# Sixteen start places for the hi and lo halves of the weights, one for each group of products

## The chip, the cores and the metric

The kernel runs on one core of one Trainium2 chip. The metric is the device time of one execution in microseconds (us); lower is better. Two executions of the kernel before took 2779.8 and 2778.5 us, median 2779.15 us. A further execution was recorded by the hardware profiler.

## What is computed

Two transformer blocks of width 2048 over 256 tokens, one after the other, each followed by its own feed-forward part. Cut to what matters here, everything is a chain of dense products with some work between them:

```python
# block 1 (x: [1, 256, 2048], all float32)
mod = silu(c) @ ada_w + ada_b                         # six vectors of 2048: shifts, scales, gates
h = rms_norm(x, g) * (1 + sc1) + sh1
u, lru_gate, q, k, v, mix_gates = split(h @ w_in + b_in)
y_lru  = rg_lru(conv(u)) * gelu(lru_gate)             # scan over the tokens
y_attn = sliding_window_attention(q, k, v, sinks)     # window 128, 16 heads, 4 kv heads
merged = sig(m0) * (y_lru @ w_lru_out) + sig(m1) * (y_attn @ w_attn_out)
x = x + g1 * (merged @ w_o)
h2 = rms_norm(x, g) * (1 + sc2) + sh2
x = x + g2 * ((silu(gate) * up) @ w_ffn_out)          # gate, up = h2 @ w_ffn_in
x = rms_norm(x, final_g)
# block 2
x = x + gla_mixer(rms_norm(x), gla_w_in, ..., gla_w_out)
x = x + swiglu(rms_norm(x), ffn_w_gu, ffn_w_down)
```

## The kernel before

**Products.** All weights are float32 in HBM, packed in chunks of 512 x 512 (1 MB, a tile `raw` of 128 partitions x 4 x 512). The large products do not run as full float32 matmuls: each operand is split into a rounded half `hi` (type float32r) and the rest `lo = raw - hi`, and three float32r matmuls, hi·hi, hi·lo and lo·hi, are added up in PSUM. `split` (L157) does this for the weights of one chunk: one DMA on the SyncE queue (SP), then for each half of the chunk one ScalarE copy to `hi` (L165) and one VectorE subtraction to `lo` (L167), 128 x 1024 elements each. `hi`, `lo` and `raw` rotate through three buffers each. The activations are held already split, as pairs of tiles (class `Pair`); they keep their places.

**Two forms.** `accumulate` (L171) issues the matmuls of one chunk. In the usual form the weights are the stationary operand, 128 columns at a time, and 256 tokens of the activations stream past: 4 x 4 x 3 = 48 matmuls of 128x256 (L189, L191, L193). With `tokens=True` the activations are stationary and 512 columns of the weights stream past: 4 x 2 x 3 = 24 matmuls of 128x512 (L182, L183, L184). The second form is used for the gate and up products of both feed-forward parts (PSUM tiles `fgps`, `fups`), for the values of the gated linear attention (`gvps`) and for one group of `w_in`. A *group* is what is accumulated into one pair of PSUM banks; its first chunk is told by `first`. Three matmuls that follow each other (hi·hi, hi·lo, lo·hi) are called a *triple* below.

**Order.** The program is written as generators which `pump()` advances once per chunk, and a scheduler fixes the order on each engine beforehand. Loads of weights have a raised priority (`lead`), so they run ahead as far as the three `raw` buffers allow.

**The strips.** `mod` is a vector-matrix product and is not done on TensorE: `matvec` (L222) loads 512 KB of `ada_w` at a time into a pool `mvw` of `MVS` = 6 buffers, and VectorE multiplies and adds it to an accumulator (L237, L239), sixteen steps to a strip; a small matmul `mvp` (L251) then sums over partitions. The loads of strip 0 are issued by SP, ahead of the first weights; those of strips 1 to 3 by GpSimd's queue (POOL) while block 1's first products run; the rest by SP again, between the weights. Each load waits until the step that last read its buffer is done. `next_h` makes the next quarter of the input `h` from each of the strips 0 to 3.

Places are given here in bytes along a partition, modulo 512. In the kernel before every `hi` and `lo` buffer begins at 128, and every 512-byte step within it stays there; the activation pairs begin at 320, and their halves 1024 bytes on.

Of the kernel before, what the change touches and what calls it, by code (L numbers as in the profile page):

```python
# [12 lines left out]
F32R = mybir.dt.float32r  # L13
# [5 lines left out]
P = 128  # L19
# [3 lines left out]
NG = NK // 4  # L23
EPS = 1e-6
PREP = 2000
SLOTS, MVS, RAWS, HIS, LOS = 24, 6, 3, 3, 3
NEG = -3.0e38
HEADS = 16
KVH = 4
# [20 lines left out]
def block_pair_kernel(ctx: ExitStack, tc: tile.TileContext, a: dict):  # L50
# [8 lines left out]
    hip = ctx.enter_context(tc.tile_pool(name="hip", bufs=HIS))  # L59
    lop = ctx.enter_context(tc.tile_pool(name="lop", bufs=LOS))  # L60
# [8 lines left out]
    def f32(ap):  # L69
        return ap.bitcast(F32)  # L70
# [79 lines left out]
    def load(ap):  # L150
        raw = rawp.tile([P, 4, 512], F32, tag="raw", name="raw")
        nc.sync.dma_start(raw, ap)
        return raw

    lead = [0]

    def split(ap):  # L157

        parts = []
        with tc.high_priority(offset=lead[0]):  # L160
            raw = load(ap)
            for b in range(2):
                rb = raw[:, 2 * b:2 * b + 2, :]
                hi = hip.tile([P, 2, 512], F32R, tag="hi", name="hi")
                nc.scalar.activation(hi, rb, AF.Copy)  # L165
                lo = lop.tile([P, 2, 512], F32R, tag="lo", name="lo")
                nc.vector.tensor_tensor(lo, rb, f32(hi), ALU.subtract)  # L167
                parts.append((hi, lo))
        return parts

    def accumulate(ps, ap, src, first, last, tokens=False):  # L171

        parts = split(ap)
        for kk in range(4):
            hi, lo = parts[kk // 2]
            wk = kk % 2
            fst, lst = first and kk == 0, last and kk == 3
            if tokens:
                for t in range(2):
                    tsl = slice(t * P, (t + 1) * P)  # L180
                    xh, xl = src.hi(kk)[:, tsl], src.lo(kk)[:, tsl]
                    nc.tensor.matmul(ps[t], xh, hi[:, wk, :], start=fst, stop=False)  # L182
                    nc.tensor.matmul(ps[t], xh, lo[:, wk, :], start=False, stop=False)  # L183
                    nc.tensor.matmul(ps[t], xl, hi[:, wk, :], start=False, stop=lst)  # L184
                continue
            for f in range(4):
                wsl = slice(f * P, (f + 1) * P)
                o = ps[f // 2][:, f % 2, :]
                nc.tensor.matmul(o, hi[:, wk, wsl], src.hi(kk), start=fst and f % 2 == 0,  # L189
                                 stop=False, skip_group_check=True)  # L190
                nc.tensor.matmul(o, hi[:, wk, wsl], src.lo(kk), start=False, stop=False,  # L191
                                 skip_group_check=True)
                nc.tensor.matmul(o, lo[:, wk, wsl], src.hi(kk), start=False, stop=lst,  # L193
                                 skip_group_check=True)
# [4 lines left out]
    def project(chunks, src, name, tokens=False):  # L199


        ps = banks(name, tokens)
        n = len(chunks)
        for c in range(n):
            accumulate(ps, chunks[c], src[c], c == 0, c == n - 1, tokens)
            if c < n - 1:
                pump()
        return ps
# [48 lines left out]
    def ada_steps(strip, queue=nc.gpsimd):  # L257


        def done(ps):  # L260
            if strip < 4:
                cols = ((16 + 4 * strip, 0, 4), (4 * strip, 4, 4))
            else:
                cols = ((8 * strip, 0, 8),)
            for j, p, n in cols:
                nc.vector.tensor_tensor(mod[:, j:j + n], ps[:, p:p + n], v("ada_b", j, n), ALU.add)

        return matvec([a["ada_w"][strip, k] for k in range(NK)], lambda k: cact[:, k:k + 1],
                      1024, done, queue)
# [149 lines left out]
    first = ada_steps(0, nc.sync)  # L419
# [36 lines left out]
    for q in range(NG):  # L456
# [3 lines left out]
        for g, ks in plan[q]:  # L460
# [7 lines left out]
            for k in ks:  # L468
                if g in held:
                    accumulate(ps, a["w_in"][g, k], h[k], k == 0, k == NG - 1, tok)  # L470
                else:
                    accumulate(ps, a["w_in"][g, k], h[k], k == ks[0], k == ks[-1])
                for st in ahead[:share]:
                    st()
                if ahead and len(ahead) <= share:
                    next_h()
                ahead = ahead[share:]
                lead[0] = PREP
                if q == NG - 1 and k < ks[-1]:
                    pump()  # L480
# [585 lines left out]
```

## Time and profile before

| | |
|---|---|
| median of the two runs | 2779.15 us |
| the profiled execution's own time | 2775.35 us |
| its span, first to last instruction | 2773.6 us |
| TensorE (PE) busy | 98% of the span |
| VectorE (DVE) / ScalarE (ACT) busy | 64% / 48% |
| mean DMA rate | 217 GB/s |
| mean granted TensorE clock | 0.999 |

A row of a group names the line, the engine, the operation, output<-inputs and the number of instructions; behind the bar stand the busy time, the mean duration of one in ns, and the idle time of the engine before them. A row of the timeline gives the start, the duration, the engine and the instruction. Matmuls are pipelined: each is shown with its whole passage, 0.28 us for one of 128x256, though the next one starts after 0.11 us. How fast the engine works is therefore read from the distance between starts, or from how many matmuls a window holds.

### The profile page before, as it was taken

What the parts mean: (1) busy time and instruction counts of PE and PEld (TensorE: products, weight loads), DVE (VectorE), ACT (ScalarE), POOL (GpSimd) and SP (SyncE); (2) the same over time, 40 slices, a digit from 0 to 9 for tenths busy, and PEclk for the clock granted to TensorE, in tenths of its full rate; (3) what the DMA queues carried; (4) which work ended last, traced back from release to release, by engine and by line L of the source; (5) the groups of instructions that cost most, each with busy time, mean ns of one, the idle gap of its engine ahead of it and who ended that gap; (6) DMA issues with size and microseconds to landing.
All of it is one profiled execution on the core that took longest, in us unless ns stands there. A gap on an engine that the chain in (4) does not pass through costs nothing.

```text
span 2773.6 us, 43912 instructions
## 1 busy us (share of the span) xinstructions
PE 2710.8 (98%) x18612; PEld 2489.2 (90%) x18612; DVE 1784.8 (64%) x2000; ACT 1321.3 (48%) x1531; POOL 25.7 (1%) x52
## 2 busy tenths in 40 slices
PE   4999999999999999999999999999999999999999
PEld 4999899999999788899888999899988889988899
DVE  8887966977876865444444677866654444444544
ACT  3446537873445444434444555555554443344443
POOL 1100000000000000000000000000000000000000
PEclk9999999999999999999999999999999999999999
DMA  9974784768875776555555544445555555555554
GB/s 364 368 301 149 261 324 175 282 241 324 326 283 181 271 259 217 180 190 193 183 192 186 190 169 168 147 144 182 192 188 182 183 190 189 198 182 189 185 196 160
DMA packets 100165, 602.00 MB, mean 217 GB/s; under 512 B 11120, under 2 KB 11632, under 8 KB 40576
## 3 DMA queue, kind: packets, MB, share of 16 engines
q1 hardware_dynamic: 93056, 574.03, 58.2%
q0 software_dynamic: 6912, 25.17, 2.3%
q8 instruction: 145, 2.38, 0.3%
q14 instruction: 52, 0.43, 0.0%
HBM read 597.06 MB, written 2.10 MB: 216 GB/s over the span
## 4 chain that ended last, share of the span: by engine, by line
PE 91%; DVE 5%; ACT 1%; issue 1%; DMA 1%; SPq 0%; DVEq 0%; ACTq 0%
PE fops L189 6%; PE fops L191 6%; PE fops L193 6%; PE fgps L184 6%; PE fgps L183 6%; PE fgps L182 6%; PE fups L184 5%; PE fups L183 5%; PE fups L182 5%; DVE lo L167 2%; PE part L189 2%; PE part L191 2%; PE part L193 2%; DVE mva L239 1%; DMA mvw<-ada_w 1%
## 5 line engine op out<-in xcount | busy, mean ns | idle before, releaser
L167 DVE TENSOR_TENSOR lo<-raw,hi 128x1024 fp32r<-128x1024 f32 x928 | 1134.4, 1223 | 899.3 <-ACT hi L165 897.5
L165 ACT ACTIVATE hi<-raw 128x1024 fp32r<-128x1024 f32 x928 | 982.8, 1060 | 1285.8 <-PE fups L184 280.6
L189 PE MATMUL fops<-hid,hi 128*128 128x256 f32 x1408 | 389.0, 276 | 0.0
L193 PE MATMUL fops<-hid,lo 128*128 128x256 f32 x1408 | 388.8, 276 | 0.0
L191 PE MATMUL fops<-hid,hi 128*128 128x256 f32 x1408 | 388.8, 276 | 0.0
L183 PE MATMUL fups<-lo,h 128*128 128x512 f32 x704 | 275.9, 392 | 0.9 <-DVE lo L167 0.9
L184 PE MATMUL fups<-hi,h 128*128 128x512 f32 x704 | 276.7, 393 | 0.0
L182 PE MATMUL fups<-hi,h 128*128 128x512 f32 x704 | 274.2, 390 | 0.0
L184 PE MATMUL fgps<-hi,h 128*128 128x512 f32 x672 | 264.9, 394 | 0.0
L182 PE MATMUL fgps<-hi,h 128*128 128x512 f32 x672 | 264.6, 394 | 0.0
L191 PEld LDWEIGHTS fops<-hid,hi 128*128 128x128 f32 x1408 | 264.3, 188 | 0.0
L189 PEld LDWEIGHTS fops<-hid,hi 128*128 128x128 f32 x1408 | 264.3, 188 | 0.0
L193 PEld LDWEIGHTS fops<-hid,lo 128*128 128x128 f32 x1408 | 264.3, 188 | 0.0
L183 PE MATMUL fgps<-lo,h 128*128 128x512 f32 x672 | 263.3, 392 | 0.0
L239 DVE SCALAR_TENSOR_TENSOR mva<-mvw,cact,mva 128x1024 f32<-128x1024 f32 x180 | 230.2, 1279 | 18.7 <-DMA mvw<-ada_w 17.0
L183 PEld LDWEIGHTS fups<-lo,h 128*128 128x128 f32 x704 | 132.2, 188 | 31.3 <-DVE lo L167 1.3
L182 PEld LDWEIGHTS fups<-hi,h 128*128 128x128 f32 x704 | 132.2, 188 | 29.3
L184 PEld LDWEIGHTS fups<-hi,h 128*128 128x128 f32 x704 | 132.3, 188 | 27.4
L183 PEld LDWEIGHTS fgps<-lo,h 128*128 128x128 f32 x672 | 126.3, 188 | 27.4
L182 PEld LDWEIGHTS fgps<-hi,h 128*128 128x128 f32 x672 | 126.3, 188 | 26.3
L184 PEld LDWEIGHTS fgps<-hi,h 128*128 128x128 f32 x672 | 126.3, 188 | 26.0
L189 PE MATMUL part<-h,hi 128*128 128x256 f32 x512 | 145.6, 284 | 0.1
(322 smaller groups left out, 5440.6 us busy)
## 6 DMA issues: line engine op xcount, KB each, us to landing
raw<-w_in SPq DMA_DIRECT2D x88, 1024.0 KB, 4.9
raw<-w_ffn_in SPq DMA_DIRECT2D x88, 1024.0 KB, 4.8
raw<-ffn_w_gu SPq DMA_DIRECT2D x88, 1024.0 KB, 4.8
mvw<-ada_w SPq DMA_DIRECT2D x144, 512.0 KB, 6.5
raw<-gla_w_in SPq DMA_DIRECT2D x48, 1024.0 KB, 4.8
raw<-w_ffn_out SPq DMA_DIRECT2D x44, 1024.0 KB, 4.9
raw<-ffn_w_down SPq DMA_DIRECT2D x44, 1024.0 KB, 4.9
mvw<-ada_w POOLq DMA_DIRECT2D x48, 512.0 KB, 8.4
```

The costliest lines, as they stand in the source:

```text
L165: nc.scalar.activation(hi, rb, AF.Copy)
L167: nc.vector.tensor_tensor(lo, rb, f32(hi), ALU.subtract)
L182: nc.tensor.matmul(ps[t], xh, hi[:, wk, :], start=fst, stop=False)
L183: nc.tensor.matmul(ps[t], xh, lo[:, wk, :], start=False, stop=False)
L184: nc.tensor.matmul(ps[t], xl, hi[:, wk, :], start=False, stop=lst)
L189: nc.tensor.matmul(o, hi[:, wk, wsl], src.hi(kk), start=fst and f % 2 == 0, stop=False, skip_group_check=True)
L191: nc.tensor.matmul(o, hi[:, wk, wsl], src.lo(kk), start=False, stop=False, skip_group_check=True)
L193: nc.tensor.matmul(o, lo[:, wk, wsl], src.hi(kk), start=False, stop=lst, skip_group_check=True)
L239: nc.vector.scalar_tensor_tensor(state["acc"], w, col(k), state["acc"], ALU.mult, ALU.add)
```

## The change

The `hi` and `lo` buffers become 128 elements longer (1152 instead of 1024 per partition, 512 bytes), and the data no longer begin at the buffer's start but at one of four places, 0, 16, 32 or 48 elements (0, 64, 128 or 192 bytes) behind it. `hi` and `lo` have places of their own, so there are sixteen combinations; `next_place` steps through them, one combination for each group, counted separately for the two forms of matmul. To make room, `MVS` goes from 6 to 5. What is multiplied with what does not change.

```diff
-SLOTS, MVS, RAWS, HIS, LOS = 24, 6, 3, 3, 3
+SLOTS, MVS, RAWS, HIS, LOS = 24, 5, 3, 3, 3
...
+    place = {}
+    groups = [0, 0]
+
+    def next_place(tokens):
+        n = groups[tokens]
+        groups[tokens] += 1
+        place["hi"], place["lo"] = 16 * (n % 4), 16 * ((n // 4 + n) % 4)
+
+    def halfbuf(pool, name):
+        t = pool.tile([P, 1024 + P], F32R, tag=name, name=name)
+        return t[:, place[name]:place[name] + 1024].rearrange("p (b n) -> p b n", b=2)
+
     def split(ap):
...
-                hi = hip.tile([P, 2, 512], F32R, tag="hi", name="hi")
+                hi = halfbuf(hip, "hi")
                 nc.scalar.activation(hi, rb, AF.Copy)
-                lo = lop.tile([P, 2, 512], F32R, tag="lo", name="lo")
+                lo = halfbuf(lop, "lo")
                 nc.vector.tensor_tensor(lo, rb, f32(hi), ALU.subtract)
...
     def accumulate(ps, ap, src, first, last, tokens=False):
 
+        if first:
+            next_place(tokens)
         parts = split(ap)
```

In bytes modulo 512, a `hi` or `lo` half now begins at 128, 192, 256 or 320; the activation pairs stay at 320, and the longer buffers (4608 bytes) still begin at 128.

The scheduler's order changes in few places; line numbers behind the insertion are 15 higher. On SP, near the end of the first products of `w_in`, stand the loads (`mvw`) of strip 4 that the free buffers allow, between loads of weights (`raw`). Before:

```order
L234 DMA mvw_3172<-ada_w 128x1024
L234 DMA mvw_3254<-ada_w 128x1024
L152 DMA raw_1825<-w_in 128x2048
L234 DMA mvw_3330<-ada_w 128x1024
L234 DMA mvw_3393<-ada_w 128x1024
L152 DMA raw_1885<-w_in 128x2048
L234 DMA mvw_3456<-ada_w 128x1024
L152 DMA raw_1948<-w_in 128x2048
L234 DMA mvw_3517<-ada_w 128x1024
```

The same place on SP with the change:

```order
L249 DMA mvw_3172<-ada_w 128x1024
L152 DMA raw_1825<-w_in 128x2048
L249 DMA mvw_3254<-ada_w 128x1024
L249 DMA mvw_3330<-ada_w 128x1024
L152 DMA raw_1885<-w_in 128x2048
L249 DMA mvw_3393<-ada_w 128x1024
L152 DMA raw_1948<-w_in 128x2048
L249 DMA mvw_3456<-ada_w 128x1024
```

Five loads run ahead instead of six, all but the first one weight load later; the sixth has moved to the next place where strip loads stand.

On PE the order is the same throughout, but for one place: the gate matmuls of the recurrence (`rps`, full float32) in the third of the four runs of `recur`, which stand between the triples of the product `gps`. Before:

```order
L193 MATMUL gps_5600<-h_618,lo_5689 128x256
L189 MATMUL gps_5600<-h_618,hi_5687 128x256
L570 MATMUL rps_5662<-uc_5580,lw_5573 128x256
L571 MATMUL rps_5662<-uc_5580,lw_5573 128x256
L191 MATMUL gps_5600<-h_618,hi_5687 128x256
L193 MATMUL gps_5600<-h_618,lo_5689 128x256
```

The same place on PE with the change:

```order
L204 MATMUL gps_5600<-h_618,hi_5687 128x256
L206 MATMUL gps_5600<-h_618,hi_5687 128x256
L585 MATMUL rps_5662<-uc_5580,lw_5573 128x256
L586 MATMUL rps_5662<-uc_5580,lw_5573 128x256
L585 MATMUL rps_5667<-uc_5580,lw_5573 128x256
L586 MATMUL rps_5667<-uc_5580,lw_5573 128x256
L208 MATMUL gps_5600<-h_618,lo_5689 128x256
```

Four pairs that stood singly between the triples now stand as two and two. On VectorE and ScalarE the strip steps and a few steps of the recurrence trade places with conversions of weights, within some five rows of where they were; GpSimd's order is the same.

## The prediction

> **What bounds the kernel now.** I read the page first, its totals and the chain that ended last.
>
> ```profile
> span 2773.6 us, 43912 instructions
> PE 2710.8 (98%) x18612; PEld 2489.2 (90%) x18612; DVE 1784.8 (64%) x2000; ACT 1321.3 (48%) x1531; POOL 25.7 (1%) x52
> ...
> PEclk9999999999999999999999999999999999999999
> ...
> PE 91%; DVE 5%; ACT 1%; issue 1%; DMA 1%; SPq 0%; DVEq 0%; ACTq 0%
> ```
>
> TensorE is busy from the first product to the end, at full granted clock, and nine tenths of the chain are its own. Next I read the list of PE's waits, whose columns are the sum in us, the number of times and the longest.
>
> ```profile
> PE mvp L251 <- DVE mva L239: 36.7, 3, 34.4
> PE e L189 <- ACT h L313: 4.4, 1, 4.4
> ```
>
> 34.4 us of this is the start, before PE has anything to do; what follows is small. So the time is the start plus the number of matmuls times the distance between their starts. The number comes from windows over the whole span for one line of each form:
>
> ```profile
> 0.00:2773.60 2773.60, 1198.10 (x4288) 806.92 (x4288) 1.00 0.61 217
> ...
> 0.00:2773.60 2773.60, 614.97 (x1568) 294.71 (x1568) 1.00 0.61 217
> ```
>
> The first row is L189, the second L182; each stands for a third of its form, so there are 4288 triples of 128x256 matmuls and 1568 of 128x512. The distance is read from the timeline of PE. In the last part, 29 matmuls of `fops` start one behind the other, of which these are the first and the last:
>
> ```profile
> 2399.73 0.28 PE L193 MATMUL fops<-hid,lo 128*128 128x256 f32 x1
> ...
> 2402.90 0.28 PE L189 MATMUL fops<-hid,hi 128*128 128x256 f32 x1
> ```
>
> 3.17 us over 28 distances is 113.2 ns. But this isn't so everywhere:
>
> ```profile
> 600.91 0.28 PE L191 MATMUL glps<-h,hi 128*128 128x256 f32 x1
> 601.02 0.28 PE L193 MATMUL glps<-h,lo 128*128 128x256 f32 x1
> 601.14 1.84 PE L251 MATMUL mvp<-ones,mva 128*128 128x1 f32 x16
> 602.84 0.36 PE L189 MATMUL glps<-h,hi 128*128 128x256 f32 x1
> 603.04 0.28 PE L191 MATMUL glps<-h,hi 128*128 128x256 f32 x1
> 603.16 0.28 PE L193 MATMUL glps<-h,lo 128*128 128x256 f32 x1
> ...
> 605.99 0.28 PE L193 MATMUL glps<-h,lo 128*128 128x256 f32 x1
> ```
>
> Up to 601 the distance is 0.11 us; sixteen small matmuls come between; from 603.04 to 605.99 there are 25 distances of 118.0 ns. Same group, same line, same places: an interruption put the stream into another, slower pattern, and it stays there. How long shows in how many instructions two long stretches hold:
>
> ```profile
> 598.00:875.00 277.00, 277.00 (x2353) 276.52 (x2352) 215.51 (x225) 122.75 (x143) 0.00 (x0) 1.00 0.79 288
> ...
> 2303.00:2434.00 131.00, 131.00 (x1157) 131.00 (x1157) 64.14 (x57) 51.20 (x51) 0.00 (x0) 1.00 0.55 192
> ```
>
> 277 / 2353 is 117.7 ns over 277 us, 131 / 1157 is 113.2 ns (a few dozen small matmuls among them change the mean little). A triple thus takes 340 or 353 ns, a step of about 13.3. The 128x512 form does the same, by fifteen rows from 1499.79 and seventeen from 155.13:
>
> ```profile
> 1499.79 0.39 PE L182 MATMUL fups<-hi,h 128*128 128x512 f32 x1
> ...
> 1503.00 0.39 PE L184 MATMUL fups<-hi,h 128*128 128x512 f32 x1
> 155.13 0.40 PE L182 MATMUL e<-hi,h 128*128 128x512 f32 x1
> ...
> 158.86 0.40 PE L183 MATMUL e<-lo,h 128*128 128x512 f32 x1
> ```
>
> 3.21 / 14 is 229.3 ns, 3.73 / 16 is 233.1: triples of 688 and 699 ns, nearly the same step. These distances are what the change could move, and the only thing that could move much.
>
> **The change part by part.** *The places.* No instruction is added, and none gets longer by its form: halves stay contiguous, 1024 elements. The start of the stationary operand (128x256 form) or of the moving one (128x512 form) shifts by 0 to 192 bytes against the activations. In the kernel before it never shifts, so no row of the large products prices it. The nearest row is the small product `lrps`, whose stationary operand `warh` steps by 16 elements, 64 bytes, from one triple to the next, and so passes through all four places of the change, while the activations stream as in the large products:
>
> ```profile
> 1646.83 0.28 PE L785 MATMUL lrps<-h,warh 128*16 128x256 f32 x1
> 1646.94 0.28 PE L786 MATMUL lrps<-h,warh 128*16 128x256 f32 x1
> ...
> 1647.96 0.28 PE L786 MATMUL lrps<-h,warh 128*16 128x256 f32 x1
> ```
>
> 1.13 us over ten distances is 113 ns, the same at each place. The caution: it loads 16 columns, not 128, and tells nothing of a shifted moving operand. I take 0, as it is the nearest row. The ends: one step of 13.3 ns worse per triple everywhere, (4288 + 1568) x 13.3 ns = +78 us, less about 10 us for the long stretch that is already slow (2353 / 3 triples), +68 us; or one step better everywhere, -78 us, of which -10 us (2353 x 4.4 ns) needs no faster pattern than the 113 ns seen.
>
> *The patterns' chance.* Since interruptions choose the pattern, and PE's order differs at one place alone (the `rps` pairs near 527 us), most stretches should fall as before. If the long one falls into the faster pattern, -10 us; if one as long as 131 us falls into the slower, 1157 x 4.4 ns = +5 us. I take 0, and these as the scatter.
>
> *The fifth buffer, at the start.* SP's queue, the DVE steps and the first conversion:
>
> ```profile
> 13.60 7.75 SPq L234 DMA_DIRECT2D mvw<-ada_w  x6
> 23.57 2.89 SPq L152 DMA_DIRECT2D raw<-w_in  x3
> 26.01 1.27 DVE L239 SCALAR_TENSOR_TENSOR mva<-mvw,cact,mva 128x1024 f32<-128x1024 f32 x1
> 40.32 2.93 ACT L165 ACTIVATE hi<-raw 128x1024 fp32r<-128x1024 f32 x3
> 44.27 0.80 PE L189 MATMUL e<-h,hi 128*128 128x256 f32 x2 [4.36 <-ACT h L313]
> 20.00:30.00 10.00, 0.00 (x0) 0.00 (x0) 9.76 (x17) 4.19 (x4) 1.19 (x2) 1.00 1.04 409
> ```
>
> The last load of strip 0 left SP by 21.35 us; with five buffers it waits for the eleventh step, which ends at 27.28, 5.9 us later. Behind it in SP's queue stand the identity, the attention mask, the first three weight chunks, `war` and `bv`. Cover: the DMA engines are full here (share 1.04), so what is issued later still comes near its turn, and the first chunk, issued at 23.57, is wanted only at 40.32. PE waits for `h` (44.27), not for weights. Between 0 and 5.9 us; I take 1, since the cover is wide.
>
> *The fifth buffer, strips 1 to 3.* Each of GpSimd's 48 loads now waits for the step five before its own instead of six before, that is for one step more:
>
> ```profile
> POOL mvw L234 <- DVE mva L239: 95.9, 45, 27.2
> 59.55 0.53 POOL L234 DMA_DIRECT2D mvw<-ada_w  x1 [2.10 <-DVE mva L239]
> 60.87 0.53 POOL L234 DMA_DIRECT2D mvw<-ada_w  x1 [0.79 <-DVE mva L239]
> 63.20 0.53 POOL L234 DMA_DIRECT2D mvw<-ada_w  x1 [1.81 <-DVE mva L239]
> 81.00 1.92 PE L251 MATMUL mvp<-ones,mva 128*128 128x1 f32 x16 [0.81 <-DVE mva L239]
> ```
>
> Issues are 1.3 to 2.3 us apart, so each load starts one such distance later. Queued behind a step that waits are DVE's `lo` conversions, and PE waits for those. What would show it is PE at `mvp` (81.00), where the last step of a strip sets PE's time: at most 2.3 us for each of three strips, +7; at least 0. I take 1. The later strips wait little for buffers:
>
> ```profile
> SPq L152 <- DVE lo L167: 2328.9, 453, 17.2
> SPq L234 <- DVE mva L239: 47.2, 28, 4.7
> ```
>
> SP spends its waiting on `raw` buffers (2328.9 us), not on `mvw` (47.2), so the fifth buffer costs nothing there; that `raw` wait covers it.
>
> *The sum.* 2775.35 (the profiled execution's own time) + 0 + 0 + 1 + 1 = 2777.4 us. The median of the runs is 3.8 us above the profiled execution, so 2781 us on that scale.
>
> **A rule that speaks against it.** The skill has a floor. The Trainium skill, "TensorE: Matmul & The Clock Gate", section "Back-to-back issue gap", gives the distance of warm matmuls as N / 2.4 + 2.5 ns, that is 109.2 and 215.8 ns; this trace disagrees, with 113.2 to 118.0 and 229.3 to 233.1 ns. By it, were the place the whole cause and the change its cure, an estimate from that page is 12,864 x 4.1 + 4704 x 13.5 ns, about 116 us less, near 2665 us. No run here shows any float32r stream at the floor.
>
> **The rivals.** *Worse places:* some combinations of places put every group that has them a step slower, whatever interrupted it. For it speaks that the step exists in both forms; against it that `lrps` doesn't change and that one place has shown both patterns. Half of the groups: 0.5 x 68 = +34, 2815 us. It decides, that is passes 2% (a gain or loss of 56 us, about what a measurement of this kernel can tell from no change), from about 4,200 triples a step slower, 72% of them; all of them: 2849 us. *Better places:* the common place before is a bad one, and the others lose a step. For it speaks that the patterns differ at all; against it the same rows. Half of the groups -39, 2742 us; 56 us needs 4,200 triples; all: 2703 us. The floor above belongs to this rival. *The buffer counts:* both ends of the fifth buffer's costs are paid, 5.9 + 7 instead of 2, +11: 2792 us. *It does nothing:* that the buffers don't move can't be; the order shows the starts.
>
> **How the numbers follow.** Places indifferent: 0.66, 2781 us, own range 2768 to 2795 (the long stretch and two of 131 us either way). The buffer counts: 0.08. Worse places: 0.16, of it 0.10 beyond 2%. Better places: 0.10, of it 0.05 beyond. So faster by over 2% 0.05, within 0.85, slower 0.10. The range from 2750 to 2815 us reaches to half of the groups worse, and on the other side to a third of them better (26 us); it leaves out about 0.18.
>
> **What would show it.** Right: the windows of long stretches hold 113 or 118 ns, with changes only behind interruptions and not with a group's place; DVE's waits for `mvw` and PE's at `mvp` grow by a microsecond or two. Wrong: distances that change from group to group with the combination and repeat after sixteen groups, or a value that wasn't there, such as 109 or 122 ns; then the place sets the pattern, and my zero for the places is the term that failed. A start of PE later than 46 us would make the first buffer term wrong.

## The result, and the profile after

The changed kernel takes 2818.49 us (median of 2814.62 and 2822.37 us) against 2779.15 us: 1.0137 times as long, interval 1.012 to 1.0154. That is 37 us more than predicted, just above the upper end of the range.

The page of the changed kernel, its span, the engines' totals and the granted clock:

```profile
span 2812.8 us, 43921 instructions
...
PE 2752.7 (98%) x18612; PEld 2523.5 (90%) x18612; DVE 1787.7 (64%) x2000; ACT 1322.2 (47%) x1531; POOL 25.7 (1%) x52
...
PEclk9999999999999999999999999999999999999999
```

TensorE has as many matmuls as before (18612), at full clock, and is busy 41.9 us longer. The span is 39.2 us longer, so nothing else needs explaining. The waits confirm it; first those of PE, then of DVE (and the same row of the kernel before) and of SP's queue (sum in us, times, longest):

```profile
PE mvp L266 <- DVE mva L254: 37.1, 3, 34.5
PE e L204 <- ACT h L328: 4.4, 1, 4.4
...
DVE mva L254 <- DMA mvw<-ada_w: 23.6, 20, 3.4
...
DVE mva L239 <- DMA mvw<-ada_w: 17.0, 13, 4.1
...
SPq L152 <- DVE lo L180: 2355.8, 452, 15.1
SPq L249 <- DVE mva L254: 59.8, 35, 4.7
```

The missing buffer is seen where it was looked for: VectorE waits for the strips' loads 23.6 us instead of 17.0, SP for free `mvw` buffers 59.8 instead of 47.2. Hardly anything of it reaches PE, which waits 37.1 us at `mvp` instead of 36.7, and starts 34.5 us in instead of 34.4. So PE's stream itself is slower. The timeline of PE at the border between two groups of `fops` shows how:

```profile
1227.36 0.28 PE L204 MATMUL fops<-hid,hi 128*128 128x256 f32 x1
...
1228.72 0.28 PE L204 MATMUL fops<-hid,hi 128*128 128x256 f32 x1
1228.84 0.28 PE L206 MATMUL fops<-hid,hi 128*128 128x256 f32 x1
...
1229.90 0.28 PE L206 MATMUL fops<-hid,hi 128*128 128x256 f32 x1
```

From the first row to the second are twelve distances, 1.36 us, 113.3 ns each. At 1228.72 a new group begins, with both places 64 bytes further, and the next ten distances, to 1229.90, take 1.18 us, 118 ns each. No other matmul and no wait stands between: the distance changes with the group. Windows of 20 us, each within one group of `fops` (start:end, length, PE busy and number of matmuls; the other engines and DMA follow), say the same:

```profile
1205.00:1225.00 20.00, 20.00 (x179) 20.00 (x178) 9.12 (x8) 7.83 (x8) 0.00 (x0) 1.00 0.53 175
1235.00:1255.00 20.00, 20.00 (x171) 20.00 (x170) 8.58 (x7) 7.49 (x8) 0.00 (x0) 1.00 0.59 207
1270.00:1290.00 20.00, 20.00 (x173) 20.00 (x172) 8.80 (x8) 7.42 (x7) 0.00 (x0) 1.00 0.55 202
...
2345.00:2365.00 20.00, 20.00 (x169) 20.00 (x168) 8.57 (x7) 7.25 (x8) 0.00 (x0) 1.00 0.59 201
2730.00:2750.00 20.00, 20.00 (x179) 20.00 (x178) 9.52 (x8) 7.44 (x7) 0.00 (x0) 1.00 0.62 211
```

`hi` and `lo` stand here at 0 and 0, 64 and 64, 128 and 128, 192 and 192, 0 and 128 bytes: 179, 171, 173, 169, 179 matmuls, with no interruption inside a window. A window also counts the two or three matmuls that began before it: 20 us at 113.3 ns are 176.5, shown as 179, and 169 stand for 120 ns. Memory traffic and the clock don't go with it: the DMA share is 0.53 and 0.62 in the two windows of 179 and 0.55 to 0.59 in the others, and the clock is 1.00 in all. The kernel before has 179 in the second of these windows too:

```profile
1235.00:1255.00 20.00, 20.00 (x179) 20.00 (x178) 10.07 (x11) 8.13 (x8) 0.00 (x0) 1.00 0.60 206
```

For all groups the following table was worked out from the starts of all matmuls of the trace: the mean time of a triple in ns (from the start of its first matmul to that of the next triple), leaving out triples with an interruption (a distance far above the others). "128x256" has the weights stationary, "128x512" has them moving. Places are in bytes within the buffer; the activations stand where place 192 does, modulo 256. (Two groups of `w_in` that are spread over the four strips, of 64 and 32 triples, have no single combination: both forms share `place`, so their later chunks take what was set last.)

| `hi` at | `lo` at 0 | 64 | 128 | 192 |
|---|---|---|---|---|
| 128x256: 0 | 343.5 | 354.7 | 340.6 | 353.3 |
| 64 | 353.9 | 356.2 | 350.2 | 355.0 |
| 128 | 347.0 | 347.1 | 353.4 | 353.3 |
| 192 | 353.4 | 357.4 | 353.3 | 359.8 |
| 128x512: 0 | 687.0 | 696.8 | 691.1 | 699.7 |
| 64 | 696.5 | 698.2 | 693.4 | 686.6 |
| 128 | 693.5 | 687.5 | 699.7 | 702.3 |
| 192 | 696.1 | 696.2 | 687.0 | 680.5 |

Most combinations have the same mean, within some 5 ns, wherever they come back: the five groups at 192 and 192 have 359 to 360 ns, the five at 0 and 128 340 to 344. Two combinations are exceptions: at 0 and 0 there are groups of 340 and of 353 ns, at 128 and 0 of 340 and of 357.

The kernel before has 0 and 0 everywhere, the second best place of the first form and a good one of the second. Summed over their starts, the 12,864 matmuls of 128x256 take 1531.1 us (before 1499.5), the 4704 of 128x512 take 1102.4 (before 1094.4): +31.6 and +8.0, together 39.6 us, the whole difference of the spans.

### The profile page after: what moved, and what is told of

The parts are those of the page before. It is cut to its first block, busy times and chain, and to the rows that moved or that the text cites. A ratio compares the mean times of both kernels' runs of the same rounds, so it can differ in the third digit from the quotient of the medians.

```text
span 2812.8 us, 43921 instructions
## 1 busy us (share of the span) xinstructions
PE 2752.7 (98%) x18612; PEld 2523.5 (90%) x18612; DVE 1787.7 (64%) x2000; ACT 1322.2 (47%) x1531; POOL 25.7 (1%) x52
## 4 chain that ended last, share of the span: by engine, by line
PE 91%; DVE 4%; DMA 2%; issue 1%; ACT 1%; POOL 0%; SPq 0%; DVEq 0%; POOLq 0%; ACTq 0%
PE fops L208 6%; PE fops L204 6%; PE fops L206 6%; PE fgps L197 6%; PE fgps L198 6%; PE fgps L199 6%; PE fups L198 5%; PE fups L197 5%; PE fups L199 5%; DVE lo L180 2%; PE part L206 2%; PE part L204 2%; PE part L208 2%; DMA mvw<-ada_w 2%; PE glps L204 1%
## 5 line engine op out<-in xcount | busy, mean ns | idle before, releaser
L204 PE MATMUL fops<-hid,hi 128*128 128x256 f32 x1408 | 394.5, 280 | 0.0
L208 PE MATMUL fops<-hid,lo 128*128 128x256 f32 x1408 | 394.5, 280 | 0.0
L206 PE MATMUL fops<-hid,hi 128*128 128x256 f32 x1408 | 393.9, 280 | 0.0
L254 DVE SCALAR_TENSOR_TENSOR mva<-mvw,cact,mva 128x1024 f32<-128x1024 f32 x180 | 230.5, 1280 | 25.3 <-DMA mvw<-ada_w 23.6
```

Of the source, the lines that this page charges most:

```text
L254: nc.vector.scalar_tensor_tensor(state["acc"], w, col(k), state["acc"], ALU.mult, ALU.add)
```

## The experiments

Two theories stood at the start. *Place*: the distance between matmuls depends on where the two weight halves begin. *Rest*: the fifth buffer, the longer buffers or the shifted order put PE's stream into its slower pattern more often, as interruptions do in the kernel before. Except where something else is said, each kernel is the changed one with its rule for places replaced by a table of (`hi`, `lo`) in elements, one row for each form:

```diff
-        place["hi"], place["lo"] = 16 * (n % 4), 16 * ((n // 4 + n) % 4)
+        table = PLACES[1 if tokens else 0]
+        place["hi"], place["lo"] = table[n % len(table)]
```

**All at one place.** Everything else of the change stays: five `mvw` buffers, longer `hi` and `lo` buffers.

```diff
+PLACES = ([(0, 0)],
+          [(0, 0)])
```

> The longer buffers and the fifth mvw buffer of the change, but all hi and lo halves at place 0, the common place of the kernel before. Theory 'place' (each combination of places has its own distance between matmuls): back to about 2780 us, 2770 to 2795, triples of 340 or 353 ns and 687 ns as before. Rival 'buffers and order' (the fifth buffer and the changed order cost the time): stays near 2818. Rival 'changing' (it is the change of place from group to group, not the place): about 2780 too; the next two runs tell that one apart.

Measured: 2779.62 us, before 2778.0 on the same chip; ratio 1.001, interval 1.0 to 1.0019. The windows in two groups of `fops` and in one stretch of the recurrence's products:

```profile
1180.00:1200.00 20.00, 20.00 (x179) 20.00 (x178) 11.03 (x12) 7.44 (x7) 0.00 (x0) 1.00 0.52 178
1240.00:1260.00 20.00, 20.00 (x178) 20.00 (x178) 10.96 (x12) 7.44 (x7) 0.00 (x0) 1.00 0.56 181
640.00:660.00 20.00, 20.00 (x172) 20.00 (x171) 15.82 (x15) 7.44 (x7) 0.00 (x0) 1.00 0.88 330
```

The groups keep one distance, and the stretch that was slow before is slow still (172, all 128x256, some 118 ns apart). So the buffers and the order cost 0 to 5 us, 1.6 by the medians, and the places, or their changing, the rest.

**The places that the map calls good.** For each form, the combination with the shortest triple:

```diff
+PLACES = ([(0, 32)],
+          [(48, 48)])
```

> As e1, but one combination for all groups of a form, the fastest ones in the profile of the change: hi 0 and lo 32 elements for the 128x256 form (triples of 340.6 ns there), hi 48 and lo 48 for the 128x512 form (680.5 ns). 'Place': against the kernel before 15 us less in the 128x256 form (no triples of 353 ns left) and 1568 x 7 ns = 11 us less in the other, so about 2754 us. 'Buffers and order': 2818. 'Changing': about 2780, as nothing changes from group to group.

Measured: 2761.73 us, ratio 0.9941, interval 0.9921 to 0.9962: faster than the kernel before, though the time is some 8 us above the expected one. Two windows in groups of `fops`, and one of 16 us in a product of 128x512:

```profile
1160.00:1180.00 20.00, 20.00 (x179) 20.00 (x178) 10.26 (x12) 8.19 (x8) 0.00 (x0) 1.00 0.55 178
1225.00:1245.00 20.00, 20.00 (x179) 20.00 (x178) 9.97 (x11) 8.40 (x8) 0.00 (x0) 1.00 0.57 185
1432.00:1448.00 16.00, 16.00 (x73) 13.23 (x72) 7.13 (x6) 7.38 (x8) 0.00 (x0) 1.00 0.58 196
```

Triples take 340.4 and 680.6 ns through the whole kernel (but for 24 of the 1568 in one of the mixed groups of `w_in`, which have the other form's place and 690.9 ns), 3.8 and 6.3 less than with all at one place. Over 4288 and 1568 triples that would be 16 and 10 us; the sums over the starts of all matmuls fell by 12.4 and 6.8. In the first form the distances of up to 130 ns between its matmuls fell by 17.5 us in all, while the hundred-odd longer ones grew from 28.0 to 33.1. Of the 12,864 matmuls of 128x256, 334 have a distance between 115.5 and 121 ns, where the kernel with all at one place has 4052 and the changed kernel 8933. So at this place hardly any interruption leaves a slow pattern behind; the two patterns of the kernel before belong to its place.

**The places that the map calls bad.**

```diff
+PLACES = ([(48, 48)],
+          [(32, 48)])
```

> As e2 with the slowest combinations: hi 48 and lo 48 for the 128x256 form (359.8 ns), hi 32 and lo 48 for the 128x512 form (702.3 ns). 'Place': 4288 x 16 ns = 69 us and 1568 x 15 ns = 23 us more than before, about 2871 us. 'Changing': about 2780. 'Buffers and order': 2818.

Measured: 2859.33 us, ratio 1.0293, interval 1.0277 to 1.0308. The same kinds of windows:

```profile
1190.00:1210.00 20.00, 20.00 (x169) 20.00 (x168) 8.42 (x8) 7.41 (x7) 0.00 (x0) 1.00 0.55 172
1265.00:1285.00 20.00, 20.00 (x169) 20.00 (x168) 10.04 (x12) 7.41 (x7) 0.00 (x0) 1.00 0.55 173
1380.00:1396.00 16.00, 16.00 (x70) 12.83 (x69) 6.70 (x6) 7.27 (x8) 0.00 (x0) 1.00 0.59 197
```

169 instead of 179, 70 instead of 73; triples of 359.9 and 703.1 ns. From the good places to the bad ones the same program, with the same instructions and buffers, gets 97.6 us slower. Nothing changes from group to group here, so it isn't the changing that costs time. It came out 12 us below the expectation for much the same reason: against all at one place the full differences would be 4288 x 15.7 and 1568 x 16.2 ns, 67 and 25 us, and the sums over the starts grew by 57.7 and 23.3. Some of the loss is taken off waits: the distances above 130 ns in the first form fell from 28.0 to 20.8 us, and at `mvp` PE waits once, at the start (34.6 us), instead of three times (37.1 us).

**Places further out.** Steps of 64 bytes up to 448, so that the pattern's period shows.

```diff
+PLACES = ([(0, 16*k) for k in range(8)] + [(16*k, 16*k) for k in range(8)],
+          [(48, 16*k) for k in range(8)] + [(16*k, 16*k) for k in range(8)])
```

> Places over 512 bytes instead of 256, by a table of sixteen combinations for each form: lo stepping from 0 to 112 elements with hi held (at 0 in the 128x256 form, at 48 in the other), then hi and lo together from 0 to 112. 'Place' with a period of 256 bytes: triples at 64 elements equal those at 0, 80 those at 16, 96 those at 32, 112 those at 48, so the same eight numbers twice. 'Place' with a period of 512 bytes or more: the second half has numbers of its own. The sum tells little here, near 2815 us either way.

Measured: 2819.96 us, one run. With `hi` at 0 and `lo` at 320, 384 and 448 bytes a 128x256 triple takes 354.7, 340.3 and 353.2 ns; at 64, 128, 192 it took 354.7, 340.6, 353.3 in the changed kernel. `lo` at 256 gives groups of 340.1 and groups of 353.3, as 0 does. With `hi` at 192 the 128x512 form gives 696.3, 696.6, 687.4, 681.0 for `lo` at 0 to 192, and 696.3, 697.6, 687.4, 681.5 for 256 to 448. With both halves at 320 and at 448, 356.9 and 359.9 ns stand against 356.2 and 359.8 at 64 and at 192. So the period is 256 bytes. Two more combinations show a second pattern here: with `hi` at 0 and `lo` at 192 one group of five has 366 ns instead of 353, and with both at 384, which is 128 modulo 256, one group has 344 instead of 353.

**Everything shifted together.** A tile of 64 bytes is put ahead of the activations; it moves the activations and also the `hi` and `lo` buffers by 64 bytes. The sixteen combinations are those of the change.

```diff
+    shift = ctx.enter_context(tc.tile_pool(name="shift", bufs=1))
+    shifted = shift.tile([P, 16], F32, name="shifted")
+    nc.gpsimd.memset(shifted, 0.0)
```

> The change, with 64 bytes set aside ahead of the pool of activations, so that activations and all behind them, the hi and lo buffers too, lie 64 bytes further; the sixteen combinations as in the change. 'Place, by the distance to the activations': each combination keeps the triple it has in the change (hi 0 lo 32: 340.6 ns; hi 48 lo 48: 359.8 ns in the 128x256 form and 680.5 ns in the other), time near 2818 us. 'Place, by the address alone': the table moves by one step, so hi 48 lo 48, now at the address that place 0 had, takes over the 340 or 353 ns and the 687 ns of hi 0 lo 0.

Measured: 2819.03 us, one run (2782.52 for the kernel before, beside it). Against the table above, 13 of the 16 values of the 128x256 form agree within 0.2 ns (the others are combinations with two patterns: 0 and 0, 341.1 instead of 343.5; 128 and 0, 346.5 instead of 347.0; 0 and 192, 357.1 instead of 353.3, as one group of four has 366), and 14 of the 16 of the 128x512 form within 1 ns (64 and 0: 690.1 instead of 696.5; 192 and 64: 694.9 instead of 696.2). Had the address itself counted, all would have moved by one row and one column. So a shift of all operands together doesn't move the table.

**Finer steps.** Steps of 16 bytes, `hi` fixed.

```diff
+PLACES = ([(0, 4*k) for k in range(16)],
+          [(48, (48 + 4*k) % 64) for k in range(16)])
```

> Steps of 4 elements, 16 bytes: hi at 0 and lo at 0, 4, 8 to 60 elements in the 128x256 form; hi at 48 and lo at 48, 52 to 60, 0, 4 to 44 in the 128x512 form. If the place counts in blocks of 64 bytes, four neighbours share a number: 340 or 353, 354.7, 340.6 and 353.3 ns, and 680.5, 696, 696 and 687 ns. If it counts by the line of 16 bytes, or by the element, the numbers lie between these or leave them; one below 340 or 680 would be a better place than any of the change. Time near 2790 us.

Measured: 2830.12 us, one run. The mean triples in ns:

```
lo at, bytes      0    16    32    48    64    80    96   112   128   144   160   176   192   208   224   240
128x256, hi 0   342.4 353.4 356.0 355.4 354.7 353.4 353.4 352.0 340.6 353.3 352.9 355.2 353.4 353.4 354.3 350.2
128x512, hi 192 696.2 696.4 693.3 696.3 698.0 700.1 696.3 694.3 687.2 693.9 699.8 692.8 680.6 695.9 694.9 706.0
```

16 bytes to either side of a good place the advantage is gone (340.6 at 128, 352.0 and 353.3 beside it; 680.6 at 192, 692.8 and 695.9 beside it). In steps of 16 bytes, and with `hi` held, the good places are single points, not ranges, and no value lies below 340 and 680.

**Short weight loads.** All matmuls but the first and last triple of an output load 16 stationary columns instead of 128, as `lrps` does, in both forms (the lines of the first are shown). So they also write only 16 of the 128 rows of their output; the rest is left out. The streams, the places and the sixteen combinations are those of the change.

```diff
+            m = P if fst or lst else 16
...
-                wsl = slice(f * P, (f + 1) * P)
-                o = ps[f // 2][:, f % 2, :]
+                wsl = slice(f * P, f * P + m)
+                o = ps[f // 2][0:m, f % 2, :]
```

> The sixteen combinations of the change, but all matmuls of a group except the first and the last of an output load 16 columns of the stationary operand instead of 128 (112 of 128 rows of their output are left out; the streams of 256 or 512 elements stay). 'A conflict between the weight load and the stream that runs beside it': with loads an eighth as long the distance no longer depends on the place, 113 ns or less and 229 or less everywhere, as in lrps; about 2780 us or less. 'The stream alone depends on its start': the 128x512 form keeps its numbers by place (680 to 702 ns), the 128x256 form, whose stream stays at one place, loses them. Neither: both keep them.

Measured: 2786.82 us, one run, before 2782.52 beside it. Windows in groups of `fops` with both halves at 64 and both at 192, then one of 128x512 with both at 192:

```profile
1225.00:1245.00 20.00, 20.00 (x174) 16.02 (x172) 8.97 (x8) 7.41 (x7) 0.00 (x0) 1.00 0.59 202
1520.00:1540.00 20.00, 20.00 (x179) 16.60 (x177) 8.62 (x8) 8.31 (x8) 0.00 (x0) 1.00 0.60 211
1425.00:1441.00 16.00, 16.00 (x71) 6.53 (x69) 6.65 (x6) 6.35 (x6) 0.00 (x0) 1.00 0.48 147
```

The worst place of the 128x256 form, 169 matmuls in 20 us, now has 179. Thirteen of its sixteen combinations come to 340.2 to 343.0 ns; three still stand out (64 and 64: 350.2, 128 and 128: 348.4, 128 and 64: 345.5). The form as a whole takes 1499.2 us, 31.9 less than in the changed kernel. The 128x512 form gains nothing: 1104.7 us, and its best place is no longer good (71 matmuls instead of 73; 690.8 instead of 680.5 ns). So in the first form most of the loss is gone with 16 columns; in the second, what a place is worth changes too, but nothing is won. As the written rows shrink along with the load, this run alone doesn't tell which of the two the loss needs.

**The best places, with the sixth buffer back.** The buffers of the halves are lengthened by 256 bytes only, which is the period, and gives the room.

```diff
-SLOTS, MVS, RAWS, HIS, LOS = 24, 5, 3, 3, 3
+SLOTS, MVS, RAWS, HIS, LOS = 24, 6, 3, 3, 3
...
-        t = pool.tile([P, 1024 + P], F32R, tag=name, name=name)
+        t = pool.tile([P, 1024 + 64], F32R, tag=name, name=name)
...
+PLACES = ([(0, 32)],
+          [(48, 48)])
```

> The places of e2 (128x256 form: hi at 0, lo at 32 elements; 128x512 form: hi and lo at 48), with the sixth mvw buffer back; the halves' buffers are 64 elements longer (256 bytes) instead of 128, which gives the room, and keeps every place the same modulo 256 bytes. Place theory: triples of 340.4 and 680.6 ns as in e2, and since the fifth buffer's absence cost 0 to 2 us in e1, 2759 to 2762 us, ratio to before 0.993 to 0.995. Rival (the places count modulo 512 bytes, and every other buffer now stands 256 bytes off): triples split by buffer, some of them 353 and 700 ns, and 2775 to 2800 us.

Measured: 2756.19 us, before 2778.12; ratio 0.9914, interval 0.9898 to 0.9929. It beats both kernels, by 0.9% the one before. Triples of 340.4 and 680.5 ns, with every other buffer 256 bytes off, so the period of 256 bytes holds. It is some 3 us better than expected; the interval meets that of the good places with five buffers only at its edge, and which part is the sixth buffer's was not tried further.

**The activations alone moved.** The weights' halves keep, modulo 256 bytes, the addresses that they have at the good places (the expectation says modulo 512; there `hi` of the first form stands at 384 instead of 128); only the activations move by 64 bytes, with the tile of 64 bytes as above and a table that takes the shift back.

```diff
+PLACES = ([(48, 16)],
+          [(32, 32)])
```

> The weights' halves stay at exactly the addresses (modulo 512 bytes) that e2 has, 128 and 256 in the 128x256 form, 320 and 320 in the 128x512 form; only the activations move, by 64 bytes, from 320 to 384. If the weights' own address sets the distance: as e2, triples of 340 and 681 ns, about 2762 us. If it is where the weights stand against the activations: the weights are now at combination (3,1) in the first form and (2,2) in the second, 355.2 and 699.8 ns in the changed kernel, so 4288 x 14.8 + 1568 x 19.2 ns = 94 us more than e2, about 2855 us.

Measured: 2849.37 us, one run, 87.6 us above the good places. The windows, as for the good places:

```profile
1190.00:1210.00 20.00, 20.00 (x170) 20.00 (x169) 8.58 (x7) 7.42 (x8) 0.00 (x0) 1.00 0.57 199
1260.00:1280.00 20.00, 20.00 (x170) 20.00 (x169) 8.56 (x8) 7.43 (x7) 0.00 (x0) 1.00 0.58 198
1434.00:1450.00 16.00, 16.00 (x70) 12.91 (x69) 7.35 (x6) 5.57 (x7) 0.00 (x0) 1.00 0.53 179
```

Triples of 357.3 and 700.0 ns, where the map of the changed kernel has 357.4 and 699.7 for the combination that the weights now form with the activations (the expectation's 355.2 is a mean without the triples of 366 ns that belong to this combination). Modulo 256 bytes no weight moved, and the gain of 16 us against the kernel before turned into a loss of 71. What counts is how the weights stand against the activations, modulo 256 bytes.

A rule, read strictly, would have said otherwise. The Trainium skill, "SBUF — State Buffer", section "Who interferes with whom", gives TensorE one read port for the moving operand and one for the weight load, calls them independent, and ends: "PE and ACT never wait on anyone." If the two reads of TensorE never disturbed each other, one would not expect it to matter where the two operands stand against each other. The runs disagree with that reading: the two kernels, whose large products modulo 256 bytes differ in nothing but that, are 88 us apart. That it is the two ports that meet is not shown.

## Why the prediction was wrong

**What bounds the kernel** was right: PE's stream, 98% of the span before and after. That its distance is the only thing which could move much was right too; all of the 39 us is there.

**The places: the step that failed.** "I take 0, as it is the nearest row", the row of `lrps`. That row loads 16 columns, and the caution against it stood beside it. The run with short loads shows that this is decisive: with 16 columns the 128x256 form is nearly the same at most places, 342.4 ns at both halves 192, where 128 columns take 359.8. The row was near in its stream, but lacked the 128 columns without which most of the effect is gone. Its two halves also step together, so that it passes through four of the sixteen combinations only, and it says nothing of the second form. The term measured +31.6 us in the first form and +8.0 in the second, instead of 0. That the time still came out only 3 us above the range is no merit of the working: the range reached that far for the sake of the rival *Worse places*.

**The ends** of that term, one step of 13.3 ns up or down everywhere, held for the sum of this change, but not for the bad places (+81 us against the kernel before, where +68 was the end); the steps are finer and reach further. Many values of the map lie near 340, 347, 353 and 360, half steps of some 6.7 ns, and the worst, 360 ns, is one and a half steps above the best. Downward the end of -78 us was out of reach: most of the kernel before already had 340, and no place gave less. From the best places with six buffers one sees what there was to win, 22 us.

**The patterns' chance** was half right. At places 0 and 0 one group has 340 ns and another 353; so also with the changed kernel's buffers. At 0 and 128 that choice is gone (334 slow distances in the whole kernel). Which interruption sets which pattern is not shown. "Same group, same line, same places" was a correct reading of two patterns at one place, and no proof that places don't matter.

**The fifth buffer at the start**, taken as 1 of 0 to 5.9 us: PE's wait at the start went from 34.4 to 34.5 us, that for `h` stayed 4.4. **Strips 1 to 3**, taken as 1 of 0 to 7: PE waits 0.4 us more at `mvp`. Both terms are small, as forecast; by these waits they are smaller than the 1 us that each was given. All at one place, the two and the order together cost 1.6 us where 2 was forecast, but the interval of 0 to 5 us doesn't tell that from nothing.

**The rivals.** *Worse places, half of the groups* gave +34 us and 2815 us; in kind it is what happened. That its number came within 4 us is luck: not half of the combinations are slower by one step, but fourteen of sixteen in the first form, by 3.5 to 16 ns against the 343.5 of the kernel before. The part of this rival that stays below 2% had 0.06 of the chance, on the word of `lrps`. *Better places* was half true as well: the common place before isn't the best, but by 0.9%, not 2.8%. *The buffer counts* was wrong, by the waits above and by the run with all at one place. The distances of 109.2 and 215.8 ns come from a formula of the Trainium skill, "TensorE: Matmul & The Clock Gate", section "Back-to-back issue gap". The prediction calls them a floor; the section calls the formula the gap of a single isolated matmul and has a lower figure, ~131 ns, for a sustained stream of N = 512. No run here reaches either: the best streams have 113.4 and 226.8 ns.

**What would show it** named the finding in advance: distances that change from group to group and come back with the combination, and a value that was hardly there before, which is 120 ns (2093 distances of the first form, 17 in the kernel before).

## What to carry to other kernels

When no row prices a change, the nearest row counts only if it has the part that the change disturbs; if it lacks it, it isn't evidence for zero, and a zero between wide ends deserves a wide range. Where a kernel is bound by TensorE's stream in float32r, measure the distance between matmuls group by group, and try the start of one operand against the other in steps of 64 bytes modulo 256: a table of two numbers was worth 22 us here, and a wrong one costs 80. A speed that varies within a kernel without waits is worth such a map before it is put down to chance.

## What the runs showed of the hardware

- The distance of float32r matmuls depends on how the places of `hi`, `lo` and the activations stand to each other modulo 256 bytes: 113.4 to 120 ns for 128x256, 226.8 to 235 ns for 128x512, as means of a combination. A common shift of 64 bytes leaves this table as it is.
- The best relation is not the same for both forms. With all operands at the same place modulo 256 the 128x256 form is at its worst (359.8 ns a triple) and the 128x512 form at its best (680.5 ns).
- Sixteen bytes are enough to lose the best place (340.6 against 352.0 and 353.3 ns).
- At some places a group takes one of two times at unchanged places: 340 or 353 ns with both halves at 0, 340 or 357 with `hi` 128 and `lo` 0, 353 or 366 with `hi` 0 and `lo` 192. At the best and the worst combination all groups of these runs are alike (340 to 345 and 358 to 361 ns). What sets the choice is not shown.
- It stays open which read waits for which. That weight loads of 16 columns remove most of it in one form and not in the other would fit the load and the stream meeting, but the rows written shrink with the columns, and no run here shows the reads themselves.
